# The 64x64 inverses of a gated DeltaNet block: lower quarter from 32x32 blocks stacked four to a tile

## The chip, the cores and the metric

The kernel runs on one core of a Trainium2 chip. The core's engines work side by side and meet through semaphores: PE (TensorE, the matrix products), DVE (VectorE), ACT (ScalarE), POOL (GpSimd) and SP (SyncE, which here only issues DMAs; ACT issues some too). The metric is the device time of one launch in microseconds (us); lower is better. All times here come from the runs and from one profiled execution of the kernel before.

## The reference

One residual block over a sequence of 1024 tokens of width 1024, in float32. With a condition vector c that gives six rows of shifts, scales and gates (`mod = silu(c) @ w_ada + b_ada`):

```
h = rms_norm(x, norm1_w) * (1 + scale1) + shift1
x = x + gate1 * (concat[gated_delta_net(h @ W_in), short_conv(h @ W_in)] @ w_out)
h = rms_norm(x, norm2_w) * (1 + scale2) + shift2
x = x + gate2 * ((silu(h @ w_gate) * (h @ w_up)) @ w_down)
out = rms_norm(x, norm_f_w)
```

The part that the change touches lies in the gated DeltaNet: 4 heads of 128 channels, the sequence cut into 16 chunks of 64 tokens. For each head and chunk

```
lmat = where(strict, (k_beta @ k.T) * decay, 0)            # 64 x 64, strictly lower
tmat = triangular_solve(lmat, eye, lower, unit_diagonal)   # inverse of (1 + lmat)
u = tmat @ v_beta
w = tmat @ (k_beta * exp(g))
```

and then a scan over the chunks carries a 128x128 state per head. With 1 + lmat written in 32x32 blocks, A11 and A22 on the diagonal and A21 below, the inverse has inv(A11) and inv(A22) on its diagonal and -inv(A22) A21 inv(A11) below it. That last block is the lower quarter of the title.

## The kernel before, in words

**Work on PE.** Nearly all products are float32 products made from pieces: a matrix is split into a rounded high part and a remainder, and three products of 128x128 by 128x512 (high by high, high by low, low by high) add up in one PSUM bank. These are the `acc<-h,u` products: the in-projection h @ W_in, eight steps of 128 of the contraction, three products each, for a column block of 128 and a half of the tokens (512). After the DeltaNet come W_out and the SwiGLU, from line L91 and L92 on.

**Two halves.** The DeltaNet runs twice, `gdn(hf)` for hf = 0 and 1, each for 512 tokens: 4 heads, and per head 4 tiles t of 128 tokens, each of which holds two chunks of 64 (c = 0, 1) side by side as a block-diagonal 128x128 matrix. In turn:

- `stage_a` per head: products of k with k give L (128x4x128: rows, tile, columns) with the sign already turned, so L holds minus lmat on its lower part and the diagonal blocks. It writes the sixteen 32x32 diagonal blocks of the head to a DRAM buffer `dl` by four DMAs, and multiplies L by the mask `offm` (L1134; in the profile `L<-L,ct`), which leaves only the block -A21 of each chunk.
- When all four heads are there, all 64 blocks are loaded into one tile A (a block per partition), inverted by a loop on DVE (L1232 to L1240), and written to the DRAM buffer `dx`: 64 rows of 1024, row h * 16 + 4 r + t for the diagonal position r and the tile t.
- `merge` per head (L1174): four DMAs put the inverted blocks of the head on the diagonal of `xbd[h]` (`xbd<-dx`); DVE transposes every 32x32 block (`Tt<-xbd`); P = L^T Tt, four products of 128 columns; an evacuation into L (`L<-P`, ACT); Q = xbd^T P, four products; DVE adds Q to Tt (`Tt<-Tt,Q`). Tt is then the transpose of tmat. DVE writes k times its factor into L (`L<-kt,bk`); u = Tt^T u and w = L^T Tt follow with their evacuations (`u<-u`, and WQ).
- The chain: for each tile and chunk the products A, K and O with the states S, and DVE and ACT work between them. Its first product is `K<-A,kt`. After it come the outputs, which end in the products `y<-ident,u`.

**What sets the order.** Up to `sim.run()` the work is written as tasks (a loader and splitter of weights, `fill`, which issues the acc products, the DeltaNet's tasks, `ada`, which makes the rows of `mod`, the evacuations). While the kernel is built, a planner (`Sim`) estimates when each instruction can start and orders tasks by priority (`merge` has 1, `fill` 9: acc products fill what is left). So the order of each engine's instructions is fixed at build time and not at run time; an engine runs its list in turn, and an instruction that isn't ready holds up all behind it. All instructions ordered this way carry the line L440 in the profile. Where a copy may go to ACT or DVE (`ecopy`) or a DMA to SP's or ACT's queue (`dma2`), the planner picks one. From L91 and L92 on the order is written by hand.

**Queues.** DMAs are issued by SP and ACT and use eight semaphores, DMAHW0 to DMAHW7, in turn over both queues: a DMA waits until the DMA that had its semaphore last has landed, and the DMAs queued behind it on the same engine wait too. Loads of weights go through a ring of five 256 KB buffers `raw` on SP; among them are those of w_ada, which DVE adds up eight in a row into `aacc` (`aacc<-raw,c_act,aacc`), ACT casts (`raw<-aacc`) and PE reduces (`ada<-raw,ones`).

Of the kernel before, what the change touches and what calls it, by code (L numbers as in the profile page):

```python
# [13 lines left out]
ALU = mybir.AluOpType  # L14
# [3 lines left out]
P = 128  # L18
# [35 lines left out]
def kernel(  # L54
# [25 lines left out]
    class Ordered:  # L80
# [18 lines left out]
    PE, DVE, ACT, POOL, SP = (Ordered(n, e) for n, e in (  # L99
        ("pe", nc.tensor), ("dve", nc.vector), ("act", nc.scalar), ("pool", nc.gpsimd), ("sp", nc.sync)))  # L100
# [30 lines left out]
    def v3(ap, a):  # L131
        return ap.rearrange("p (a b) -> p a b", a=a)

    def flat(ap):
        return ap.rearrange("p a b -> p (a b)")

    def bc2(col, n):
        return col.unsqueeze(2).to_broadcast([col.shape[0], col.shape[1], n])

    def bc1(row, n):  # L140
        return row.unsqueeze(1).to_broadcast([row.shape[0], n, row.shape[1]])
# [53 lines left out]
    def dma2(out, in_):  # L195
        kw = dict(out=out, in_=in_)
        mover[0].either([("sp", "dma_start", nc.sync.dma_start, (), kw), ("act", "dma_start", nc.scalar.dma_start, (), kw)])
# [98 lines left out]
    class Sim:  # L296
# [18 lines left out]
        def free(self, t):  # L315
            res, i = self.owner.pop(t.tensor.name)
            res.slots.append((max([a[4] for a in self.acc.get(t.tensor.name, [])] + [0.0]), i))
            res.slots.sort()
# [205 lines left out]
    tri, blk, mL, mU, offm = (ct[:, i * P:(i + 1) * P] for i in range(5))  # L524
# [16 lines left out]
    sim = Sim(seq, dict(pe=T_START[0], dve=T_START[1], act=T_START[2], pool=T_START[3], sp=T_START[4]))  # L541
# [8 lines left out]
    dense, chb = sim.res("b", 3), sim.res("b", 5, (6, 7, 3, 4, 5))  # L550
# [6 lines left out]
    def bank(res, name):  # L557
        return res.tile(psp, [P, HT], F32, name)

    def gt(tag, shape=(P, 4, P), dtype=F32):  # L560
        return GP[tag].tile(gp, list(shape), dtype, tag)
# [4 lines left out]
    free = sim.free  # L566

    def ecopy(dst, src):
        sim.either([("act", "copy", nc.scalar.copy, (dst, src), {}), ("dve", "tensor_copy", nc.vector.tensor_copy, (dst, src), {})])
# [9 lines left out]
    def mm(out_, lhsT, rhs, start=True, stop=True):  # L579
        PE.matmul(out_, lhsT, rhs, start=start, stop=stop)  # L580
# [5 lines left out]
    done = set()  # L586
# [483 lines left out]
    xbd, S = [], {}  # L1070
    sw = lambda ap: ap.rearrange("p t (c n) -> p t c n", c=2)
    tsl = lambda t: slice(t * P, (t + 1) * P)
# [21 lines left out]
    def stage_a(hf, h, dl, T, dec):  # L1094
# [5 lines left out]
        at, L, WQ, egl = (dec[h][n] for n in ("at", "L", "WQ", "egl"))  # L1100
# [30 lines left out]
        DVE.tensor_tensor(bv, rk, hcol("beta"), ALU.mult)  # L1131
        for t in (nk, rk, av, nav):
            free(t)
        DVE.tensor_tensor(L, L, bc1(offm, 4), ALU.mult)  # L1134
        DVE.tensor_tensor(qd, v3(qv, 4), qd, ALU.mult)
        pqk = bank(chb, "qk")
        for t in range(4):
# [36 lines left out]
    def merge(hf, h, T, dx):  # L1174
        st, t_ = sc_[hf], T[h]
        u = us[hf]
        for r in range(4):
            dma2(xbd[h][32 * r:32 * r + 32, :, 32 * r:32 * r + 32],
                dx[h * 16 + r * 4:h * 16 + r * 4 + 4, :].rearrange("t (a b) -> a t b", a=32))
        Tt = gt("Tt")  # L1180
        sim.wait(lambda: ("a", hf, h) in done)
        DVE.transpose(flat(Tt), flat(xbd[h]))
        pP = bank(chb, "P")
        for t in range(4):
            mm(pP[:, tsl(t)], t_["L"][:, t, :], Tt[:, t, :])
        ecopy(flat(t_["L"]), pP)
        free(pP)
        pQ = bank(chb, "Q")
        for t in range(4):
            mm(pQ[:, tsl(t)], xbd[h][:, t, :], t_["L"][:, t, :])  # L1190
        DVE.tensor_tensor(flat(Tt), flat(Tt), pQ, ALU.add)
        free(pQ)
        DVE.tensor_tensor(t_["L"], t_["kt"], bc2(t_["bk"], P), ALU.mult)
        free(t_["bk"])
        sim.wait(lambda: ("vt", hf, h) in done)
        pu = bank(chb, "u")
        for t in range(4):
            mm(pu[:, tsl(t)], Tt[:, t, :], u[:, h, t, :])
        ecopy(flat(u[:, h]), pu)
        free(pu)  # L1200
        pw = bank(chb, "w")
        for t in range(4):
            mm(pw[:, tsl(t)], t_["L"][:, t, :], Tt[:, t, :])
        free(t_["L"])
        free(Tt)
        ecopy(t_["WQ"].rearrange("p t (c n) -> p t c n", c=4)[:, :, 0:4:3, :],
                 pw.rearrange("p (t c n) -> p t c n", t=4, c=2))
        free(pw)
        DVE.tensor_tensor(t_["kt"], t_["kt"], bc2(st["kd"][:, :, h], P), ALU.mult)
        done.add(("uw", hf, h))  # L1210

    def gdn(hf):
# [10 lines left out]
        for h in heads:  # L1223
            sim.spawn(decays, PR["a"], hf, h, rows, dec)
            sim.spawn(stage_a, PR["a"], hf, h, dl, T, dec)
            sim.spawn(stage_v, PR["v"], hf, h, T)
# [17 lines left out]
        for h in heads:  # L1244
            sim.spawn(merge, PR["m"], hf, h, T, dx)
# [467 lines left out]
    c = {p: {} for p in range(NP)}  # L1713
# [435 lines left out]
```

## Time and profile before

| what | value |
|---|---|
| median of 3 runs (lowest to highest) | 1187.25 us (1186.67 to 1187.44) |
| the profiled execution's own time | 1186.41 us |
| its span in the trace | 1184.6 us |
| mean granted TensorE clock | 0.998 |
| PE busy | 1171.7 us (99%) |
| DVE, ACT, POOL busy | 928.4, 528.4, 55.6 us |
| merges of the first half, the second half | from about 196 us, from about 377 us |
| static order (L91, L92) begins | 490 us |

The median stands 0.84 us above the profiled execution, and 1.8 us of that execution's time lie outside its span.

How to read the lines below. A group of instructions reads: line, engine, operation, out<-in by the program's names (for a product 128*128 is the size of the stationary operand), partitions x elements and type, x count | busy us, mean ns of one | idle time of the engine just before them, and what ended most of it. A timeline row has the start, the time to the end of the last of its instructions, the engine and what ran. A product leaves one record for each pass, and a product in plain float32 has two passes. Records of PE overlap in its pipe, so the mean of one is more than the distance between two starts. A row by stretches gives for each engine busy time and instructions in that stretch, then the granted clock (PEclk), the DMA share and GB/s. A DMA row gives the queue, the number, KB each and the median us from issue to landing. A row of waits of PE reads: who waits <- for whom: us in total, times, the longest.

### The profile page before, as it was taken

What the parts mean: (1) busy time and instruction counts of PE and PEld (TensorE: products, weight loads), DVE (VectorE), ACT (ScalarE), POOL (GpSimd) and SP (SyncE); (2) the same over time, 40 slices, a digit from 0 to 9 for tenths busy, and PEclk for the clock granted to TensorE, in tenths of its full rate; (3) what the DMA queues carried; (4) which work ended last, traced back from release to release, by engine and by line L of the source; (5) the groups of instructions that cost most, each with busy time, mean ns of one, the idle gap of its engine ahead of it and who ended that gap; (6) DMA issues with size and microseconds to landing.
All of it is one profiled execution on the core that took longest, in us unless ns stands there. A gap on an engine that the chain in (4) does not pass through costs nothing.

```text
span 1184.6 us, 16797 instructions
## 1 busy us (share of the span) xinstructions
PE 1171.7 (99%) x5723; PEld 984.3 (83%) x5723; DVE 928.4 (78%) x1739; ACT 528.4 (45%) x1117; POOL 55.6 (5%) x95
## 2 busy tenths in 40 slices
PE   8999999999999999999999999999999999999997
PEld 7888888988888988888888888888888888888886
DVE  6998989799978789658787677767767697688676
ACT  3498732359642545125443333333333355433343
POOL 1010000001000001100000000000000000000003
PEclk9999999999999999999999999999999999999999
DMA  9934465544424546632354655455644679869413
GB/s 290 301 77 120 125 179 160 160 116 137 112 47 114 154 121 206 260 98 81 133 168 142 222 188 179 153 175 187 224 155 133 222 280 395 306 203 343 146 37 142
DMA packets 175775, 207.08 MB, mean 175 GB/s; under 512 B 21829, under 2 KB 107978, under 8 KB 175690
## 3 DMA queue, kind: packets, MB, share of 16 engines
q1 hardware_dynamic: 170312, 202.85, 53.7%
q10 hardware_dynamic: 5378, 3.16, 0.9%
q8 instruction: 45, 0.74, 0.3%
q14 instruction: 40, 0.33, 0.1%
HBM read 150.91 MB, written 55.05 MB: 174 GB/s over the span
## 4 chain that ended last, share of the span: by engine, by line
PE 95%; DVE 2%; DMA 1%; ACT 1%; issue 0%; SPq 0%; DVEq 0%; ACTq 0%
PE acc L91 34%; PE acc L440 26%; PE dn L91 17%; PE o L91 4%; PE o L440 4%; PE A L440 1%; PE K L440 1%; PE ab L440 1%; PE Q L440 1%; PE u L440 1%; PE w L440 1%; PE P L440 1%; PE kk L440 1%; PE qk L440 1%; DMA wr<-in_w_in_dram 1%; PE O L440 1%
## 5 line engine op out<-in xcount | busy, mean ns | idle before, releaser
L440 PE MATMUL acc<-h,u 128*128 128x512 f32 x1200 | 302.6, 398 | 0.0
L440 PEld LDWEIGHTS acc<-h,u 128*128 128x128 f32 x1200 | 219.0, 188 | 41.2
L91 PE MATMUL acc<-h,hl 128*128 128x512 f32 x600 | 140.1, 390 | 0.0
L91 PEld LDWEIGHTS acc<-h,hl 128*128 128x128 f32 x600 | 112.4, 188 | 23.2
L91 PE MATMUL acc<-h,u 128*128 128x512 f32 x456 | 106.1, 389 | 0.0
L91 PE MATMUL acc<-T,hl 128*128 128x512 f32 x432 | 101.3, 390 | 0.2 <-ACT cc L92 0.2
L91 PEld LDWEIGHTS acc<-h,u 128*128 128x128 f32 x456 | 85.6, 188 | 17.7
L91 PEld LDWEIGHTS acc<-T,hl 128*128 128x128 f32 x432 | 80.9, 188 | 17.2 <-ACT cc L92 0.6
L92 DVE TENSOR_TENSOR xo<-xo,dn 128x512 f32<-128x512 f32 x84 | 57.1, 684 | 44.1 <-PE dn L91 36.2
L91 PE MATMUL dn<-h,h 128*128 128x512 f32 x396 | 90.7, 389 | 0.0
L91 PEld LDWEIGHTS dn<-h,h 128*128 128x128 f32 x396 | 74.3, 188 | 15.4
L92 ACT COPY cc<-acc 128x512 f32<-128x512 f32 x66 | 38.4, 590 | 108.4 <-PE acc L91 108.4
L91 PE MATMUL acc<-T,u 128*128 128x512 f32 x360 | 84.0, 389 | 0.0
L91 PEld LDWEIGHTS acc<-T,u 128*128 128x128 f32 x360 | 67.6, 188 | 14.0
L440 ACT CAST u<-raw 128x512 fp32r<-128x512 f32 x64 | 39.8, 622 | 70.9 <-PE acc L440 61.1
L92 DVE TENSOR_TENSOR cc<-cc,acc 128x512 f32<-128x512 f32 x66 | 43.8, 683 | 29.8 <-PE acc L91 29.8
L440 DVE TENSOR_TENSOR u<-raw,u 128x512 fp32r<-128x512 f32 x82 | 56.1, 684 | 12.6 <-ACT u L440 11.8
L92 DVE TENSOR_TENSOR hl<-R,hl 128x512 fp32r<-128x512 f32 x60 | 39.4, 688 | 33.4 <-ACT hl L92 33.4
L440 DVE SCALAR_TENSOR_TENSOR cv<-pr,cols_b,cv 128x512 f32<-128x512 f32 x72 | 53.1, 746 | 1.3 <-ACT cv L440 0.9
L92 ACT CAST h<-rw 128x512 fp32r<-128x512 f32 x57 | 32.7, 617 | 41.0 <-PE dn L91 34.6
L92 ACT CAST hl<-R 128x512 fp32r<-128x512 f32 x60 | 35.7, 620 | 24.7 <-DVE R L92 10.7
L92 DVE TENSOR_TENSOR u<-R,u 128x512 fp32r<-128x512 f32 x46 | 30.1, 687 | 20.5 <-ACT u L92 20.5
(336 smaller groups left out, 2026.2 us busy)
## 6 DMA issues: line engine op xcount, KB each, us to landing
raw<-in_w_in_dram SPq DMA_DIRECT2D x82, 256.0 KB, 3.4
am_scr<-cc SPq DMA_DIRECT2D x77, 256.0 KB, 4.5
raw<-in_w_ada_dram SPq DMA_DIRECT2D x56, 256.0 KB, 3.3
rw<-am_scr SPq DMA_DIRECT2D x55, 256.0 KB, 5.1
rw<-bm_scr SPq DMA_DIRECT2D x53, 256.0 KB, 5.3
bm_scr<-raw SPq DMA_DIRECT2D x51, 256.0 KB, 5.5
R<-in_w_gate_dram SPq DMA_DIRECT2D x22, 512.0 KB, 4.3
R<-in_w_up_dram SPq DMA_DIRECT2D x22, 512.0 KB, 5.4
```

The costliest lines, as they stand in the source:

```text
L91: return call(*a, **k)
L92: ins = call(*a, **k)
L440: ins = call(*a, **k)
```

## The change

The mask of L in `stage_a` is gone: only the blocks -A21 are read from L now. A `merge` works with 32x32 blocks instead of block-diagonal 128x128 tiles:

- CB holds the blocks -A21, four on the diagonal of a 128x128 tile: chunks c = 0, 1 of the two tiles t = p + 2g, p = 0, 1. Two such tiles (g = 0, 1) make a head, written by four copies of 32x2x32 from L.
- Two DMAs bring the inverted A22 blocks into the columns 32 to 63 of L's first two tiles, stacked in the same way in the partition direction, and two DVE transposes of 128x32 turn them.
- Four DMAs bring the inverted A11 blocks on the diagonal of XA, as CB is; four DMAs fill X as `xbd[h]` was filled before.
- P is two products of 32 columns (CB stationary, the transposed A22 blocks moving); one copy of 128x64 brings it into L; Q is two products of 32 columns (XA stationary); four copies of 32x2x32 put Q's blocks into the upper right quarter of each chunk of Tt. Tt is DVE's transpose of X, and nothing is added to it.

A step and head thus has two products of 32 columns where it had four of 128, and ten DMAs where it had four. Heads h and h + 2 share the tiles `xbd[h % 2]` (X) and `xbd[2 + h % 2]` (XA and CB), so the merge of head h + 2 begins only after the products Q of head h are issued. In all, the built program has 5268 products instead of 5300, and 80 DMAs from dx instead of 32.

```diff
@@ -1131,7 +1131,6 @@
         DVE.tensor_tensor(bv, rk, hcol("beta"), ALU.mult)
         for t in (nk, rk, av, nav):
             free(t)
-        DVE.tensor_tensor(L, L, bc1(offm, 4), ALU.mult)
         DVE.tensor_tensor(qd, v3(qv, 4), qd, ALU.mult)
         pqk = bank(chb, "qk")
         for t in range(4):
@@ -1174,22 +1173,38 @@
     def merge(hf, h, T, dx):
         st, t_ = sc_[hf], T[h]
         u = us[hf]
+        X, L = xbd[h % 2], t_["L"]
+        XA, CB = xbd[2 + h % 2][:, 0:2, :], xbd[2 + h % 2][:, 2:4, :]
+        sim.wait(lambda: h < 2 or ("xb", hf, h - 2) in done)
+        slots_ = [(c, p, slice(32 * (2 * c + p), 32 * (2 * c + p) + 32)) for c in range(2) for p in range(2)]
+        for c, p, sl in slots_:
+            ecopy(CB[sl, :, sl], L[64 * c + 32:64 * c + 64, p:4:2, 64 * c:64 * c + 32])
+        for c in range(2):
+            dma2(L[64 * c:64 * c + 64, 0:2, 32:64],
+                 dx[h * 16 + 8 * c + 4:h * 16 + 8 * c + 8, :].rearrange("(g p) (a b) -> (p a) g b", p=2, a=32))
+        for c, p, sl in slots_:
+            r0 = h * 16 + 8 * c + p
+            dma2(XA[sl, :, sl], dx[r0:r0 + 3:2, :].rearrange("g (a b) -> a g b", a=32))
         for r in range(4):
-            dma2(xbd[h][32 * r:32 * r + 32, :, 32 * r:32 * r + 32],
+            dma2(X[32 * r:32 * r + 32, :, 32 * r:32 * r + 32],
                 dx[h * 16 + r * 4:h * 16 + r * 4 + 4, :].rearrange("t (a b) -> a t b", a=32))
+        for g in range(2):
+            DVE.transpose(L[:, 2 + g, 32:64], L[:, g, 32:64])
+        pP = bank(chb, "P")
+        for g in range(2):
+            mm(pP[:, 32 * g:32 * g + 32], CB[:, g, :], L[:, 2 + g, 32:64])
+        ecopy(L[:, 0:2, 96:128], v3(pP[:, 0:64], 2))
+        free(pP)
         Tt = gt("Tt")
+        DVE.transpose(flat(Tt), flat(X))
+        pQ = bank(chb, "Q")
+        for g in range(2):
+            mm(pQ[:, 32 * g:32 * g + 32], XA[:, g, :], L[:, g, 96:128])
+        done.add(("xb", hf, h))
+        for c, p, sl in slots_:
+            ecopy(Tt[64 * c:64 * c + 32, p:4:2, 64 * c + 32:64 * c + 64], v3(pQ[sl, 0:64], 2))
+        free(pQ)
         sim.wait(lambda: ("a", hf, h) in done)
-        DVE.transpose(flat(Tt), flat(xbd[h]))
-        pP = bank(chb, "P")
-        for t in range(4):
-            mm(pP[:, tsl(t)], t_["L"][:, t, :], Tt[:, t, :])
-        ecopy(flat(t_["L"]), pP)
-        free(pP)
-        pQ = bank(chb, "Q")
-        for t in range(4):
-            mm(pQ[:, tsl(t)], xbd[h][:, t, :], t_["L"][:, t, :])
-        DVE.tensor_tensor(flat(Tt), flat(Tt), pQ, ALU.add)
-        free(pQ)
         DVE.tensor_tensor(t_["L"], t_["kt"], bc2(t_["bk"], P), ALU.mult)
         free(t_["bk"])
         sim.wait(lambda: ("vt", hf, h) in done)
```

The orders below name each tile with its number. In the first half P_423 and so on are results of P, L_221 to L_224 the L tiles of heads 0 to 3, xbd2 and xbd3 hold XA and CB, and raw_N are weight loads. First PE, from where P of head 0 stands, before:

```order
L440 MATMUL acc_415_2237<-h7_1_181_1000,u_392_2083 128x512 x3
L440 MATMUL acc_426_2296<-h0_0_45_272,u_404_2160 128x512 x3
L440 MATMUL acc_426_2296<-h1_0_53_333,u_404_2160 128x512 x3
L440 MATMUL P_427_2300<-Tt_420_2264,L_221_1185 128x128 x4
L440 MATMUL acc_426_2296<-h2_0_60_377,u_404_2160 128x512 x2
L440 MATMUL P_430_2315<-Tt_423_2281,L_222_1186 128x128 x4
```

and after:

```order
L440 MATMUL acc_419_2251<-h7_1_181_1000,u_395_2090 128x512 x3
L440 MATMUL P_423_2299<-L_221_1185,xbd2_1049 128x32 x2
L440 MATMUL acc_426_2310<-h0_0_45_272,u_407_2164 128x512 x3
L440 MATMUL acc_426_2310<-h1_0_53_333,u_407_2164 128x512 x3
L440 MATMUL Q_429_2327<-L_221_1185,xbd2_1049 128x32 x2
L440 MATMUL acc_426_2310<-h2_0_60_377,u_407_2164 128x512 x2
L440 MATMUL P_430_2335<-L_222_1186,xbd3_1050 128x32 x2
```

P of head 0 moved ahead of six acc products; the merges of the four heads that stood close together now stretch over 29 acc products, up to the product w of head 2, whose place is:

```order
L440 MATMUL acc_446_2461<-h0_1_138_793,u_407_2164 128x512
L440 MATMUL u_448_2470<-u_297_1522,Tt_439_2421 128x128 x3
L440 MATMUL acc_446_2461<-h0_1_138_793,u_407_2164 128x512
L440 MATMUL acc_446_2461<-h1_1_143_808,u_407_2164 128x512 x2
L440 MATMUL w_450_2489<-Tt_439_2421,L_223_1187 128x128 x4
```

This w reads L_223 (head 2), and u_448 reads Tt_439, head 2's Tt.

SP's queue at the same place, before, with what each DMA waits for in brackets (the engines' names stand for their semaphores):

```order
L440 DMA xbd2_1049<-dx_213_1169 32x4x32 [waits DMAHW4_49]
L440 DMA xbd3_1050<-dx_213_1169 32x4x32 [waits DMAHW6_49,Pool_49]
L440 DMA xbd3_1050<-dx_213_1169 32x4x32 [waits DMAHW0_49]
L440 DMA raw_422_2278<-in_w_in_dram 128x4x128 [waits DMAHW1_49,PE_49,Activation_49]
L440 DMA raw_421_2272<-in_w_ada_dram 128x512 [waits DMAHW2_49,Activation_49]
```

and after, from the last DMA of SP's first wave (heads 0 and 1) into the second wave (heads 2 and 3):

```order
L440 DMA xbd1_1048<-dx_213_1169 32x4x32 [waits DMAHW5_49]
L440 DMA raw_424_2302<-in_w_in_dram 128x4x128 [waits DMAHW7_49,DMAHW0_49,DVE_49]
L440 DMA raw_422_2277<-in_w_ada_dram 128x512 [waits DMAHW0_49]
L440 DMA raw_431_2337<-in_w_in_dram 128x4x128 [waits DMAHW2_49,DMAHW1_49,DVE_49]
L440 DMA L_223_1187<-dx_213_1169 64x2x32 [waits DMAHW3_49]
L440 DMA L_223_1187<-dx_213_1169 64x2x32 [waits DMAHW5_49]
L440 DMA xbd2_1049<-dx_213_1169 32x2x32 [waits DMAHW7_49,DMAHW6_49,PE_49]
L440 DMA xbd2_1049<-dx_213_1169 32x2x32 [waits DMAHW1_49]
L440 DMA xbd0_1047<-dx_213_1169 32x4x32 [waits DMAHW2_49,DVE_49]
L440 DMA xbd0_1047<-dx_213_1169 32x4x32 [waits DMAHW3_49]
L440 DMA raw_435_2381<-in_w_ada_dram 128x512 [waits DMAHW5_49]
L440 DMA L_224_1188<-dx_213_1169 64x2x32 [waits DMAHW6_49]
```

Three rows further, SP's queue after the change ends the second wave and goes on with weight loads:

```order
L440 DMA xbd3_1050<-dx_213_1169 32x2x32 [waits DMAHW4_49]
L440 DMA xbd1_1048<-dx_213_1169 32x4x32 [waits DMAHW5_49,DVE_49]
L440 DMA xbd1_1048<-dx_213_1169 32x4x32 [waits DMAHW6_49]
L440 DMA raw_441_2429<-in_w_ada_dram 128x512 [waits DMAHW7_49]
L440 DMA raw_447_2463<-in_w_ada_dram 128x512 [waits DMAHW0_49,DVE_49]
L440 DMA raw_449_2482<-in_w_ada_dram 128x512 [waits DMAHW1_49,DVE_49]
```

The small DMAs that followed one another before now have weight loads between them and take turns with them on the eight semaphores: xbd2's first waits for raw_424 on DMAHW7, its second for raw_431 on DMAHW1, xbd1's first for raw_435 on DMAHW5.

DVE at the place where head 2's L is filled, before:

```order
L440 TENSOR_TENSOR kt_274_1387<-kt_274_1387,kd_203_1118 128x512
L440 TENSOR_TENSOR Tt_424_2289<-Tt_424_2289,Q_438_2362 128x512
L440 TENSOR_TENSOR L_223_1187<-kt_290_1469,bk_320_1626 128x512
L440 TENSOR_TENSOR Tt_428_2303<-Tt_428_2303,Q_442_2381 128x512
L440 TENSOR_TENSOR L_224_1188<-kt_336_1731,bk_354_1800 128x512
L440 SCALAR_TENSOR_TENSOR aacc_416_2245<-raw_444_2394,c_act_112,aacc_416_2245 128x512
```

and after:

```order
L440 STREAM_TRANSPOSE Tt_444_2453<-xbd1_1048 128x512
L440 SCALAR_TENSOR_TENSOR aacc_415_2217<-raw_441_2429,c_act_112,aacc_415_2217 128x512
L440 TENSOR_TENSOR L_223_1187<-kt_284_1460,bk_316_1605 128x512
L440 TENSOR_TENSOR cv_420_2259<-acc_426_2310,cv_420_2259 128x512
L440 SCALAR_TENSOR_TENSOR aacc_415_2217<-raw_447_2463,c_act_112,aacc_415_2217 128x512
L440 TENSOR_TENSOR L_224_1188<-kt_332_1701,bk_349_1768 128x512
```

Steps of aacc, which read weight loads, moved ahead of the filling of L for heads 2 and 3.

In the second half ACT's order after the change has, near the merge of heads 2 and 3:

```order
L440 COPY L_557_2963<-P_777_4309 128x2x32
L440 CAST h5_0_774_4275<-raw_762_4216 128x512
L440 COPY u_654_3440<-u_779_4327 128x512
L440 COPY Tt_781_4334<-Q_782_4336 32x2x32 x2
L440 COPY WQ_564_2970<-w_786_4353 128x4x2x64
```

The cast of raw_762, a load of y from scratch memory on SP, stands between an evacuation of P and the copies of u and Q.

## The prediction

> **What bounds the kernel now.** I read four views in this order: the page's busy times, busy time by stretch of the span, the waits of PE, then PE's groups and timeline in the stretch that the change touches.
>
> ```profile
> PE 1171.7 (99%) x5723; PEld 984.3 (83%) x5723; DVE 928.4 (78%) x1739; ACT 528.4 (45%) x1117; POOL 55.6 (5%) x95
> 60.00:480.00 420.00, 420.00 (x2281) 359.68 (x2280) 369.56 (x853) 230.48 (x578) 29.04 (x33) 1.00 0.47 134
> PE acc L91 <- ACT cc L92: 0.2, 1, 0.2
> ```
>
> PE is busy for 99% of the span, and from 60 to 480 us, where both halves' merges lie, for all 420 us at a granted clock of 1.00. Its waits from 60 to 600 us are one of 0.2 us. So PE's instruction stream is the time: what the change takes from PE counts fully, and what it adds on DVE (370 of those 420 us busy), ACT (230) or the DMA queues counts only where PE comes to wait. The sum therefore has two kinds of term: PE time saved, and new PE waits.
>
> **PE time saved.** The two products of a merge, and the nearest rows to a narrow product:
>
> ```profile
> L440 PE MATMUL P<-Tt,L 128*128 128x128 f32 x64 | 8.8, 275 | 0.0
> L440 PE MATMUL Q<-L,xbd 128*128 128x128 f32 x64 | 8.4, 275 | 0.0
> 341.10 41.55 PE L440 MATMUL acc<-h,u 128*128 128x512 f32 x182
> 382.49 2.84 PE L440 MATMUL P<-Tt,L 128*128 128x128 f32 x24
> 385.16 1.95 PE L440 MATMUL Q<-L,xbd 128*128 128x128 f32 x16
> 96.05 0.52 PE L440 MATMUL G<-g,ct 128*128 128x16 f32 x4
> 96.41 0.31 PE L440 MATMUL abt<-ident,raw 128*128 128x128 f32 x1
> 11.12 1.02 PE L440 MATMUL ada<-c_act,wa 128*128 128x1 f32 x8 [0.36 <-DMA wa<-in_w_ada_dram]
> 12.01 0.91 PE L440 MATMUL tr<-ident,x 128*128 128x128 f32 x4
> ```
>
> Records overlap in the pipe, so I price them by the distance between starts. Each fp32 product of 128 columns leaves two records. 24 records of P take 385.16 - 382.49 = 2.67 us, 0.111 each, so the 128 records removed are worth 14.2 us. The 64 new ones (two products, two passes, two steps, eight merges) have 32 moving columns but still 128 stationary ones. The rows on both sides of 32 columns are G with 16 (four records in 0.36 us, 0.09 each) and, as the upper end, P itself with 128 (0.111); ada with one column pays that too (eight in 0.89). So 5.8 to 7.1 us stay, and 7.1 to 8.4 are saved. I take 7.1: one column costs as much as 128 in two of these three rows, and the narrow products stand scattered between acc products.
>
> The Trainium skill ("TensorE: Matmul & The Clock Gate", "Back-to-back issue gap") gives products of 1 to 64 columns a gap of about 25 ns, and its section "LDWEIGHTS (loading the stationary operand)" about 107 ns for any load of 128 stationary columns. The rows above agree with the second. By the first, the 64 records would be an estimated 1.6 us and the saving 12.6.
>
> **Work off PE.** DVE loses eight masks and eight additions and gains 16 transposes of 128x32; ACT's eight evacuations of P shrink, and some 65 copies of 32x2x32 and 48 small DMAs are added.
>
> ```profile
> L440 DVE TENSOR_TENSOR L<-L,ct 128x512 f32<-128x512 f32 x8 | 5.5, 686 | 1.0 <-DMA dl<-L 0.9
> L440 DVE TENSOR_TENSOR Tt<-Tt,Q 128x512 f32<-128x512 f32 x8 | 5.5, 682 | 1.7 <-PE Q L440 1.7
> L440 DVE COPY ablo<-abt 128x32 f32<-128x32 f32 x2 | 0.4, 182 | 0.0
> L440 ACT COPY L<-P 128x512 f32<-128x512 f32 x8 | 4.7, 588 | 10.3 <-PE P L440 10.3
> L440 ACT COPY S<-K 128x128 f32<-128x128 f32 x4 | 0.8, 280 | 1.7 <-PE K L440 1.7
> ```
>
> DVE: 16 x 0.68 = 11 us less; 16 transposes and some ten copies at about 0.18 (ablo, 32 columns) are 4.7 more. ACT: 55 copies between 0.18 and 0.28 (S) are 10 to 15 us more, 8 x about 0.3 less for the smaller L<-P, and 24 issues at 0.46 (SP's rate, below) are 11 more. DVE's slack of 50 us and ACT's of 190 from 60 to 480 hide this as work. Its cost, if any, is lateness inside a merge.
>
> **New waits, first half.** Here the DMAs decide. T0 is the landing of dx.
>
> ```profile
> 193.03 0.46 SPq L440 DMA_DIRECT2D dx<-A  x1
> 196.06 4.14 SPq L440 DMA_DIRECT2D xbd<-dx  x9
> dx<-A SPq DMA_DIRECT2D x1, 256.0 KB, 2.9
> xbd<-dx SPq DMA_DIRECT2D x9, 16.0 KB, 1.9
> raw<-in_w_in_dram SPq DMA_DIRECT2D x82, 256.0 KB, 3.4
> raw<-in_w_ada_dram SPq DMA_DIRECT2D x56, 256.0 KB, 3.3
> 200.93 1.05 PE L440 MATMUL P<-Tt,L 128*128 128x128 f32 x8
> 201.73 0.71 PE L440 MATMUL acc<-h,u 128*128 128x512 f32 x2
> L440 DVE SCALAR_TENSOR_TENSOR aacc<-raw,c_act,aacc 128x512 f32<-128x512 f32 x49 | 36.5, 744 | 3.2 <-DMA raw<-in_w_ada_dram 3.0
> L440 DVE TENSOR_TENSOR L<-kt,bk 128x512 f32<-128x512 f32 x8 | 5.5, 683 | 0.0
> 218.93 1.05 PE L440 MATMUL K<-A,kt 128*128 128x128 f32 x8
> ```
>
> T0 = 193.03 + 2.9 = 195.9. Before, all 16 small DMAs go out at once (nine on SP at 4.14 / 9 = 0.46 each), and P of head 0 starts at T0 + 5.0. In the new order six acc products fewer stand ahead of it; one costs 41.39 / 182 = 0.227, so PE reaches it at T0 + 3.6, when the A22 blocks, in the first DMAs after dx, have had 1.9 us to land and been transposed.
>
> Now the DMAs come in two waves, since heads 2 and 3 reuse the tiles of heads 0 and 1, and the rows of SP in the part on the change show what lies between: 256 KB weight loads. A DMA waits for the landing of the one eight before it. SP's first wave (ten at 0.46) ends at T0 + 4.6. Then raw_424, raw_422 and raw_431 go out at 4.7, 5.2 and 5.7 and two blocks of L_223 by 7.0. The first xbd2 row waits for raw_424 (4.7 + 3.4 = 8.1), the next for raw_431 (9.1). xbd0 twice to 10.8, raw_435 at 10.9, L_224 and xbd3 to 13.3; xbd1 waits for raw_435 (10.9 + 3.3 = 14.2), and raw_441 goes out behind it at 15.1 and lands at 18.4. DVE's order has aacc<-raw_441 (0.74) ahead of L_223<-kt,bk (0.68), which w of head 2 reads: ready at 19.8. From P(0) to that w PE has 29 acc products (6.6 us), 20 products u and w of 128 columns (40 x 0.111 = 4.4) and 16 narrow ones (3.0): due at 3.6 + 14.0 = 17.6. **PE waits about 2.3 us there**, for a weight load that has nothing to do with the merge. Behind it the same chain runs once more (raw_449, aacc, a cast to raw, copies of u, A), and I allow 0.7 for it:
>
> ```profile
> L440 ACT CAST raw<-aacc 128x512 fp32r<-128x512 f32 x6 | 3.7, 618 | 4.5 <-DVE aacc L440 2.4 <-issue 1.8 <-DVE pr L440 0.4
> L440 ACT COPY u<-u 128x512 f32<-128x512 f32 x8 | 4.7, 587 | 5.1 <-PE u L440 5.0
> ```
>
> First half: 3.0 us, between 0 (loads a little quicker, or fillers that reach) and 7.2 (the last rival).
>
> **Second half.** Here the merge meets loads of y from scratch memory. The nearest load from scratch memory is:
>
> ```profile
> Tt<-z_scr SPq DMA_DIRECT2D x3, 256.0 KB, 4.7
> ```
>
> T0' is the second dx's landing. On SP raw_762 stands behind the first wave and waits of the same kind and goes out by my count at T0' + 10.5; it lands 4.7 later, at 15.2. ACT's order has its cast (0.62) ahead of a copy of u (0.59) and of copies of Q into Tt (two of about 0.2), so the last is done at 16.8, and u of head 2 needs it at 15.7 to 16.4. I take 0.5, between 0 (a load at 3.3) and 3.3 (below).
>
> The Trainium skill (the same page, "Part 1: The HAM clock gate") says that PE falls to half clock after an idle window of about 3.4 us. The stretch above has 1.00 with no such idle, so no run here shows it; a wait of 3.0 us would be near that bound, and one beyond it would cost an estimated 2 to 4 us more at half speed.
>
> Last, the end of this part: the chain's last O, the last y and the first product of the static order.
>
> ```profile
> 445.49 1.05 PE L440 MATMUL O<-A,at 128*128 128x128 f32 x8
> 462.18 0.60 PE L440 MATMUL y<-ident,u 128*128 128x128 f32 x4
> 490.41 0.40 PE L91 MATMUL o<-L,WQ 128*128 128x512 f32 x1
> ```
>
> 28 us lie between y and the static order, full of products that don't need the chain, so a chain that is some us late is not waited for there.
>
> **Sum.** -7.1 + 3.0 + 0.5 = -3.6 us. Against the profiled execution's own 1186.41 us that is 1182.8; the median of the runs is 0.84 above that execution, so **1183.6 us** against 1187.25.
>
> **Rivals.**
> - *The waits are covered.* For it: before, PE waited 0.0 at P and Q although the loads share the queues. Then 1187.25 - 7.1 = 1180.2, or 1178.9 with G's price. Against: raw_441 didn't stand in a merge before.
> - *The waits eat the saving*: 4 to 7 us of them, 1184.9 to 1188.
> - *Loads in series are slow; slower than before.* Place: the weight loads that the second wave waits for. The loads of z_scr in that very stretch took 4.7 us. At 4.7 instead of 3.3 each of the three in series in the first half adds 1.4, 3.0 + 4.2 = 7.2 us; two in the second half make 0.5 + 2.8 = 3.3. Together 10.5, 1187.25 - 7.1 + 10.5 = 1190.6. It decides from a mean wait of 3.55 us per half (no gain), and is visibly slower from 4.75. Against: 138 of these loads took 3.3 to 3.4 as the median.
> - *Narrow products cost almost nothing.* Against it stand the rows of ada and G, which pay 0.09 to 0.11 for one and 16 columns. If a record took a quarter of G's 0.09, 64 would be 1.4, the saving 12.8, and with the waits 1187.25 - 12.8 + 3.5 = 1177.9. The first rule of the Trainium skill named above would make it so.
>
> **How the numbers follow.** 0.2% of this kernel, 2.4 us, is about what a measurement can tell from no change: faster is below 1184.9, slower above 1189.6. Chances: the forecast (waits of 1 to 5 us in all, 1181 to 1185.2) 0.45; covered (about 1180) 0.24; eaten (1185 to 1189) 0.13; slower 0.15; narrow products nearly free 0.03. Faster holds 0.03, 0.24 and a part of the forecast's 0.45, some 0.37: 0.64. Slower is the fourth, 0.15; the rest, 0.21, lies between. The range 1179 to 1188.5 leaves out the fast end of two cases (0.05) and the slower one (0.15).
>
> **What the profile after would show.** P and Q with 64 records, the distance between starts of adjacent ones 0.09 to 0.111. PE waits between 190 and 222 us, the longest at w or u of heads 2 and 3, released by DVE's L<-kt,bk or ACT's u copy, whose own wait is for raw<-in_w_ada_dram. Elsewhere no new waits. Wrong would I be if xbd DMAs land far later than 1.9 us, if PE waits at P or Q of heads 0 and 1, if the granted clock falls below 1.00 in that stretch, or if the difference lies after 490 us.

## The result, and the profile after

The changed kernel takes 1187.82 us in the median of 13 runs (1186.21 to 1188.93), the kernel before 1187.75 us in runs beside it. The ratio is 1.0001 with a 95% interval of 0.9994 to 1.0008, so by the interval the change moves the time by something between -0.7 and +0.9 us. The forecast was 1183.6, faster by 3.6 us. The products did get cheaper by about what was reckoned; all of it was given back.

First the changed kernel's page and its busy time by stretches:

```profile
PE 1170.2 (99%) x5659; PEld 978.0 (83%) x5659; DVE 928.2 (78%) x1763; ACT 527.0 (44%) x1157; POOL 56.2 (5%) x95
```

```profile
60.00:480.00 420.00, 417.30 (x2220) 352.61 (x2219) 367.56 (x877) 229.99 (x619) 31.00 (x32) 1.00 0.47 134
```

PE's waits from 60 to 600 us, where there was one of 0.2 us before:

```profile
PE P L440 <- DVE L L440: 1.5, 3, 0.9
PE Q L440 <- ACT L L440: 0.7, 2, 0.4
PE y L440 <- DVE u L440: 0.2, 1, 0.2
PE w L440 <- DVE L L440: 0.2, 1, 0.2
PE acc L91 <- ACT cc L92: 0.2, 1, 0.2
```

PE has 64 records fewer and stands idle for 2.7 us of a stretch in which it had never been idle. The groups of the two products, after (before, they are in the prediction):

```profile
L440 PE MATMUL Q<-L,xbd 128*128 128x32 f32 x32 | 4.6, 262 | 0.7 <-ACT L L440 0.7
L440 PE MATMUL P<-L,xbd 128*128 128x32 f32 x32 | 4.5, 264 | 1.6 <-DVE L L440 1.5
```

P and Q fell from 17.2 us busy to 9.1. Busy time counts tails that overlap in the pipe, so I also added up, over the trace from the first acc product to the static order, the distance from each record of PE to the next start. P and Q have 13.9 us before and 6.8 after, 7.1 less. The records that are the same in both kernels have 6.3 more: acc 3.0, w 1.2, o 0.9, the others 1.3 together. PE's waits stand in these distances (one at P lies in the distance of the acc product ahead of it).

Most of the 6.3 us is lateness, and it is more than the rows of waits show. From 60 to 484 us PE stops eleven times, where before it never did. Set against the median distance of records with the same neighbours, the distances that hold a stop are 4.6 us longer: 2.7 that the profile counts as idle and 1.9 more, some 0.17 at each stop. Distances without an idle time are another 1.8 us longer than before, and the profile names no wait for those. The switches between plain float32 and acc products, which cut up the merges now (before, their products stood in rows of 8 to 24 records), are not what costs: there are 202 of them before and 208 after in that stretch. By the medians the record ahead of a plain float32 product takes 0.233 us for 0.227 and the first plain one behind it 0.108 for 0.111; on the way back the last plain one takes 0.031 for 0.112 and the first acc product behind it 0.315 for 0.227. Together that is 0.01 us.

Where the time stands in each kernel can be read from three points: the two writes of dx on SP, which end the two solves, and PE's first product of the static order. Before, then after:

```profile
193.03 0.46 SPq L440 DMA_DIRECT2D dx<-A  x1
373.80 0.47 SPq L440 DMA_DIRECT2D dx<-A  x1
490.41 0.40 PE L91 MATMUL o<-L,WQ 128*128 128x512 f32 x1
```

```profile
193.47 0.47 SPq L440 DMA_DIRECT2D dx<-A  x1
373.17 0.48 SPq L440 DMA_DIRECT2D dx<-A  x1
490.26 0.40 PE L91 MATMUL o<-L,WQ 128*128 128x512 f32 x1
```

| stretch | before, us | after, us | difference |
|---|---|---|---|
| start to the first dx | 193.03 | 193.47 | +0.44 |
| first dx to second dx (first merges) | 180.77 | 179.70 | -1.07 |
| second dx to the static order (second merges) | 116.61 | 117.09 | +0.48 |
| static order to the end of the span | 694.19 | 694.44 | +0.25 |

The three points cut PE's list a little differently in the two kernels: after the change three acc products more and one of ada fewer start between the two writes, and one acc product fewer behind the second. With 0.24 us for each, the same products gained 1.5 us in the first half and lost 0.7 in the second, where each half was to save half of 7.1. So 2.0 us of that were given back in the first half and 4.3 in the second. In the second half PE's longest waits in the merges are, in the timeline of the changed kernel:

```profile
383.53 0.63 PE L440 MATMUL Q<-L,xbd 128*128 128x32 f32 x4 [0.41 <-ACT L L440]
390.75 0.60 PE L440 MATMUL P<-L,xbd 128*128 128x32 f32 x4 [0.85 <-DVE L L440]
395.23 0.60 PE L440 MATMUL P<-L,xbd 128*128 128x32 f32 x4 [0.39 <-DVE L L440]
```

DVE at that time:

```profile
389.84 0.43 DVE L440 CAST h<-raw 128x512 fp32r<-128x512 f32 x1
390.39 0.30 DVE L440 STREAM_TRANSPOSE L<-L 128x32 f32<-128x32 f32 x2
...
394.87 0.30 DVE L440 STREAM_TRANSPOSE L<-L 128x32 f32<-128x32 f32 x2 [1.77 <-DMA L<-dx]
```

And the queues of ACT (the first row) and SP:

```profile
383.38 0.61 ACTq L440 DMA_DIRECT2D L<-dx  x1
383.49 1.01 SPq L440 DMA_DIRECT2D raw<-in_w_in_dram  x2
385.32 0.59 SPq L440 DMA_DIRECT2D L<-dx  x1
388.43 1.85 SPq L440 DMA_DIRECT2D xbd<-dx  x4
391.28 1.24 SPq L440 DMA_DIRECT2D L<-dx  x2
```

P of head 2 (390.75) and P of head 3 (395.23) wait for the transposes of their A22 blocks, and both times the transposes start 0.02 us after the later of the two DMAs that bring the blocks has landed. By the marks of the DMAs' semaphores in the trace, SP's DMA of 385.32 landed at 390.37, and the second of the two of 391.28 at 394.85. DVE had been free for 0.1 us when the first of these landed, so it isn't its casts that PE waited for. What was late is the small DMAs themselves: all DMAs issued from 383.4 to 385.4 us, three loads of 256 KB and five small ones of the second wave, took 4.6 to 5.2 us to land. SP stood from 385.9 to 388.4 because its next DMA waited for the semaphore of one of these small ones (ACT's of 383.38, landed at 388.36), and so the blocks of head 3 left SP only at 391.28. The DMAs from issue to landing in the stretch 373 to 400, in medians:

```profile
raw<-in_w_in_dram SPq DMA_DIRECT2D x5, 256.0 KB, 5.0
L<-dx SPq DMA_DIRECT2D x5, 16.0 KB, 2.8
L<-dx ACTq DMA_DIRECT2D x3, 16.0 KB, 5.0
```

In the first half, the place that the prediction had worked out is there too: w of head 2 at 216.58, with T0 = 196.4 (the start of the first DMA from dx) at T0 + 20.2 where 19.8 was forecast, released by DVE's L, which follows the step of aacc that waited for a load (PE, then DVE):

```profile
216.58 1.16 PE L440 MATMUL w<-Tt,L 128*128 128x128 f32 x8 [0.17 <-DVE L L440]
```

```profile
215.17 0.75 DVE L440 SCALAR_TENSOR_TENSOR aacc<-raw,c_act,aacc 128x512 f32<-128x512 f32 x1 [0.84 <-DMA raw<-in_w_ada_dram]
215.84 0.68 DVE L440 TENSOR_TENSOR L<-kt,bk 128x512 f32<-128x512 f32 x1
```

PE's wait there is 0.17 us and not 2.3, because PE itself was late: from P of head 0 to its arrival at this w it took 16.2 us (200.20 to 216.41) where 14.0 were reckoned. Of the 2.2 us more, 0.56 are its waits at Q of head 0 and P of head 3; the rest are longer distances between records.

### The profile page after: what moved, and what is told of

It reads as the page before. It is cut to its first block, busy times and chain, and to the rows that moved or that the text cites. A ratio compares the mean times of both kernels' runs of the same rounds, so it can differ in the third digit from the quotient of the medians.

```text
span 1184.7 us, 16801 instructions
## 1 busy us (share of the span) xinstructions
PE 1170.2 (99%) x5659; PEld 978.0 (83%) x5659; DVE 928.2 (78%) x1763; ACT 527.0 (44%) x1157; POOL 56.2 (5%) x95
## 4 chain that ended last, share of the span: by engine, by line
PE 86%; DVE 5%; DMA 4%; ACT 1%; issue 1%; ACTq 1%; SPq 0%; POOL 0%; DVEq 0%; POOLq 0%
PE acc L91 34%; PE acc L440 21%; PE dn L91 17%; PE o L91 4%; PE o L440 3%; DMA raw<-in_w_out_dram 1%; DMA raw<-in_w_in_dram 1%; DVE raw L440 1%; DMA xbd<-dx 1%; PE ada L440 1%; PE ab L440 1%; PE K L440 1%; PE qk L440 1%; PE kk L440 1%; DMA raw<-in_w_ada_dram 1%
## 5 line engine op out<-in xcount | busy, mean ns | idle before, releaser
L91 PEld LDWEIGHTS acc<-T,hl 128*128 128x128 f32 x432 | 80.9, 188 | 17.2 <-ACT cc L92 0.6
L440 ACT CAST u<-raw 128x512 fp32r<-128x512 f32 x60 | 37.2, 623 | 57.3 <-PE acc L440 50.3
```

The source lines that it names most:

```text
L91: return call(*a, **k)
L440: ins = call(*a, **k)
```

## The experiments

All were timed against the kernel before on the same chip (5 to 12 runs of each); the microseconds are the ratio's distance from 1 times 1187. Waits are those of one profiled execution, which can lie up to 2.2 us from the median of its kernel (1184.26 against 1182.07 in the first run below). The 4.4 us of waits in the changed kernel's merges that some expectations name come near to the 4.6 by distances above; by the rows of waits, as given below, they are 2.4. Theory W: the narrow products save what was reckoned, and what the new transfers and copies make late in the merges gives it back. Rivals: N, narrow products save little; A, ACT's queue is to blame; S, what counts is the order that the planner builds, and switching between kinds of products.

**The narrow products alone.** The kernel before, with

```diff
-        for t in range(4):
-            mm(pP[:, tsl(t)], t_["L"][:, t, :], Tt[:, t, :])
-        ecopy(flat(t_["L"]), pP)
+        for g in range(2):
+            mm(pP[:, 32 * g:32 * g + 32], t_["L"][:, g, :], Tt[:, g, 32:64])
+        ecopy(flat(t_["L"]).rearrange("p (a b) -> p a b", b=64), bc1(pP[:, 0:64], 8))
```

and the like for Q and the addition.

> The kernel before with P and Q cut to two products of 32 columns each and nothing else changed: masks, DMAs, copies and additions keep their sizes (they read the 64 columns eight times over), so the kernel leaves three quarters of both products out. Theory W (the narrow products save PE 6 to 7.4 us, and the waits that the new transfers and copies bring into the merges, 4.4 us in the changed kernel's trace, and some smaller ones give it back): 6 to 7 us faster than before, 1181 to 1182, and PE waits in the merges under 1 us. Rival N (the narrow products save little, since each still loads 128 stationary columns and stands alone among acc products): no more than 2 us faster, and the changed kernel's waits are beside the point.

Ratio 0.9959 (0.9947 to 0.9971): 4.9 us faster, 3.4 to 6.3. P and Q cost as in the changed kernel, with no wait before them:

```profile
L440 PE MATMUL Q<-L,xbd 128*128 128x32 f32 x32 | 4.6, 261 | 0.0
L440 PE MATMUL P<-Tt,L 128*128 128x32 f32 x32 | 4.5, 262 | 0.0
```

N falls. The gain is below the 6 to 7 expected: the profiled execution has about 1.5 us of new waits elsewhere (two for the states' S at A, one each at K, ada and w).

**Everything but the narrowness.** The changed kernel with four products of 128 columns:

```diff
-            mm(pP[:, 32 * g:32 * g + 32], CB[:, g, :], L[:, 2 + g, 32:64])
+            for r in range(2):
+                mm(pP[:, tsl(2 * r + g)], CB[:, g, :], L[:, 2 + g, :])
```

> The changed kernel with four products of 128 columns again for P and for Q, of the same stacked operands, of which the same blocks as before are used; its DMAs, copies and transposes are untouched. 64 more records at 0.111 and 64 dearer by 0.005 are 7.4 us more work on PE. Theory W: the waits end when data arrive, so part of the added work fills them: 3 to 6 us slower than the changed kernel, 1191 to 1194, with waits in the merges of 1 to 3 us. Rival N: within 2 us of the changed kernel.

Ratio 1.0045 (1.0033 to 1.0057): 5.3 us slower than before, 3.9 to 6.8. Its waits:

```profile
PE P L440 <- DVE L L440: 1.4, 2, 1.1
PE u L440 <- DVE Tt L440: 0.5, 1, 0.5
PE ada L440 <- ACT raw L440: 0.4, 1, 0.4
```

With the run before it this splits the change, the planner's order of each included: the narrow products bring 4.9 us, the stacking (48 more DMAs, two waves, some 65 copies, 16 transposes) costs 5.3, and both together were measured as 0.1 slower.

**The mask alone.** The kernel before without `DVE.tensor_tensor(L, L, bc1(offm, 4), ALU.mult)`.

> The kernel before without the mask of L and with nothing else of the change, so that the products P read unmasked blocks of L. Theory W: DVE isn't the bound, eight instructions of 0.69 us less on it are worth nothing by themselves; the planner builds a somewhat other order, which may move the time by up to 1.5 us either way: 1185.5 to 1188.5. Rival S (what the changed kernel loses comes from the order that the planner builds whenever costs change a little): this one moves by 2 us or more as well.

Ratio 0.9996 (0.9988 to 1.0005), PE never idle in the merges. DVE's saved work is worth nothing, as priced; a small change of the order did no harm here.

**All small DMAs on SP.** In `merge`, `dma2(` became `dma(` throughout.

> The changed kernel with all ten DMAs of a merge on SP's queue, none on ACT's. Rival A (the waits come from ACT: its evacuations of P and Q stand behind the ten DMA issues in its own queue, 0.39 and 0.53 us at Q of head 0): those two waits vanish and the time falls by 1 to 2.5 us to 1185.5 to 1187. Theory W (it is the landing of the second wave of small DMAs, late because they take turns with weight loads): SP has twice the issues, 0.46 to 0.6 us each, the second wave lands later still, and the time stays or rises by up to 3 us, 1187.5 to 1191.

Ratio 1.0069 (1.0055 to 1.0083), 8.2 us slower. The wait at Q went, and eight others came:

```profile
PE A L440 <- DVE S L440: 1.7, 3, 0.9
PE K L440 <- DVE A L440: 1.4, 2, 0.9
PE P L440 <- DVE L L440: 1.1, 2, 0.6
PE O L440 <- ACT A L440: 1.1, 1, 1.1
PE acc L440 <- ACT u L440: 0.9, 1, 0.9
```

So A was right about the wait and wrong about the time: with 17 or 18 more issues on SP in each half, PE waits in the chain (A, K, O) and once at an acc product for its weights. Part of the 8.2 us is the clock. Behind the waits in the chain the granted clock (the number ahead of the DMA share) was at half for 6.8 us:

```profile
445.30:448.70 3.40, 1.57 (x11) 1.14 (x10) 3.40 (x8) 2.24 (x4) 0.00 (x0) 1.00 0.99 269
448.70:452.20 3.50, 2.44 (x10) 1.93 (x11) 3.42 (x7) 1.06 (x3) 0.00 (x0) 0.51 1.04 414
452.20:455.60 3.40, 3.40 (x13) 3.01 (x13) 3.17 (x6) 2.99 (x14) 0.00 (x0) 0.50 0.98 372
```

PE was busy for 2.44 + 3.40 us there; at full clock that work would have taken about half, so the estimate is up to 2.9 us in this execution.

**Later landings in the plan.** The planner's rule for a DMA of a merge:

```diff
                     end = rd = self.pipe + DMA_T[1]
+                    if task["name"] == "merge":
+                        end = rd = end + 1.5
```

> The changed kernel, built with the planner told that every DMA of a merge lands 1.5 us later than it reckoned, so that it puts more acc products ahead of P and Q; no instruction is added or removed. Theory W: the waits in the merges fall from 4.4 us to 1 or 2, and the time to 1184 to 1186. Rival S (the saving is lost to switching between fp32 products and acc products, and to the order elsewhere, not to waits in the merges): unchanged, 1187 to 1189.

Ratio 0.9985 (0.9977 to 0.9994), 1.8 us faster than before. The sign is W's, but not the reason given: the profiled execution has 4.3 us of waits in the merges, more than the 2.4 of the changed kernel, at Q, w and u instead of P (at 1186.68 it stands 1.2 us above the median of its runs):

```profile
PE Q L440 <- ACT L L440: 1.7, 1, 1.7
PE w L440 <- DVE L L440: 1.6, 1, 1.6
PE u L440 <- DVE Tt L440: 1.0, 1, 1.0
```

The control with 0.5 in place of 1.5:

> A control: the changed kernel, built with the planner told that the DMAs of a merge land 0.5 us later than it reckoned (1.5 in the earlier run). The order of the merges and of what lies between them changes, the work does not. If the orders of the runs with later landings gained because they wait for real landings: between the changed kernel and the run with 1.5, 1185.5 to 1187.5. If any new order moves the time by chance (as the run with P's evacuation on DVE suggests, 3 to 4 us above the one that it was made from): anything from 1183 to 1190, with waits in other places than those of the changed kernel.

Ratio 0.9988 (0.9979 to 0.9997), 1.4 us faster, between the two as the first branch has it; its interval overlaps that of 1.5, so the two can't be told apart. Its waits (P 1.5, u 1.9, y 0.4, Q 0.3) stand in part at other places than the changed kernel's, as the second branch has it. So a gain by chance of the order isn't ruled out.

**One wave.** Each head has its own XA and CB, X's blocks land in Tt:

```diff
-        X, L = xbd[h % 2], t_["L"]
-        XA, CB = xbd[2 + h % 2][:, 0:2, :], xbd[2 + h % 2][:, 2:4, :]
-        sim.wait(lambda: h < 2 or ("xb", hf, h - 2) in done)
+        L = t_["L"]
+        XA, CB = xbd[h][:, 0:2, :], xbd[h][:, 2:4, :]
+        Tt = gt("Tt")
+        POOL.memset(Tt, 0.0)
...
-            dma2(X[32 * r:32 * r + 32, :, 32 * r:32 * r + 32],
+            dma2(Tt[32 * r:32 * r + 32, :, 32 * r:32 * r + 32],
...
-        DVE.transpose(flat(Tt), flat(X))
+        DVE.transpose(flat(Tt), flat(Tt))
```

> The changed kernel without the sharing of tiles between heads h and h + 2: each head has its own tile for XA and CB, and the blocks of X land in Tt itself (set to zero by POOL before), which DVE transposes in place. All 40 small DMAs of a half go out at once, ahead of the weight loads. If the waits come from the second wave of DMAs taking turns with loads: those at P of heads 2 and 3 go, PE waits 1 to 2 us in all in the merges, and the time is 1183 to 1185.5. If they come from the small DMAs as such (20 issues of 0.5 to 0.6 us on each queue, ahead of loads and copies): no faster than the changed kernel, 1186.5 to 1190.

Ratio 0.9982 (0.9973 to 0.999), 2.1 us faster. The A22 blocks land earlier, in the same stretch from 373 to 400 us:

```profile
L<-dx SPq DMA_DIRECT2D x4, 16.0 KB, 2.2
L<-dx ACTq DMA_DIRECT2D x4, 16.0 KB, 2.1
```

And the waits at P are gone:

```profile
PE ada L440 <- ACT raw L440: 1.3, 1, 1.3
PE y L440 <- DVE so L440: 1.0, 1, 1.0
PE Q L440 <- ACT L L440: 0.5, 2, 0.3
```

Those at ada and y, 2.3 us, lie outside the merges; the changed kernel had 0.2 at y.

**One wave and later landings** (both edits).

> One wave as above, and the planner told that the DMAs of a merge land 1.5 us later than it reckoned. If the rest of the waits is the planner's too early landing: 1 to 2 us below the run with one wave, 1181.5 to 1184. If not: the same within 1 us, as the later order of the changed kernel gained only 1 to 2 us.

Ratio 0.9971 (0.996 to 0.9981), 3.4 us faster, median 1183.99: the best of all runs with the whole computation, and better than both kernels. Waits at Q 1.2 and u 0.3.

**Transposed blocks from DRAM.** One wave, with

```diff
+        for k, b_ in enumerate((tmp, gt("Tt", (64, 512)))):
+            DVE.tensor_copy(b_.rearrange("p (a b) -> p a b", a=16), A[:, :, 16 * k:16 * k + 16].rearrange("p a b -> p b a"))
+            dma(dt_[:, 512 * k:512 * k + 512], b_)
```

and the merges' transposes taken out.

> One wave as in the run with own tiles, and DVE's transposes gone too: after the solve DVE writes the transposed blocks once (two copies of 64x512) to a second DRAM buffer, from which A22 and Tt's blocks are read already transposed. If DVE's place in the chain from landing to P and u (transposes behind casts of late loads) makes waits of its own, they vanish: 1181.5 to 1184, below the run with one wave by 1 to 2 us. If the landing alone decides, the two copies and one more DMA of 2.9 us put everything later by about 2 us while acc products fill the time: equal to the run with one wave within 1 us.

Ratio 1.001 (1.0001 to 1.0019), 1.2 us slower than before and 3.3 slower than one wave: the later landing is not covered; PE waits 2.4 us at u and 1.7 at Q. Neither branch had it that bad. Taking the transposes off DVE gained nothing here, which fits the trace above, where they started as soon as the blocks had landed.

**Copies in place of six DMAs.** One wave, with A22 and A11 copied from X by `ecopy`; then the same with later landings.

> The run with one wave, but six of a merge's ten DMAs replaced by copies inside SBUF: only X's four blocks are read from DRAM (16 small DMAs in a half, as in the kernel before), and A22 and A11 are copied from them by eight copies of 32x2x32 on ACT or DVE. If the number of small DMAs is what costs (issue time on ACT ahead of its evacuations, weight loads pushed back by 20 issues on SP): 1 to 3 us below the run with one wave, 1181.5 to 1183.5. If the copies, 0.2 us each and in the chain from landing to P, cost as much as they save: 1184 to 1187, with the waits now at P for ACT's or DVE's copies.

> The same with copies, and the planner told that the DMAs of a merge land 1.5 us later than it reckoned. If the planner's estimate of landings still makes PE wait: 0.5 to 1.5 us below the run with copies alone. If not: the same within 1 us.

Ratios 0.9998 (0.9989 to 1.0008) and 0.9999 (0.9991 to 1.0008). As many small DMAs as the kernel before had, and no gain: PE's waits in the merges are 0.4 and 0.2 us, but others stand at ada, A, K and y (1.5 and 2.7 us), and the first has a stretch at half clock (last section); the granted clock of its runs is lower as a whole (table below). So these two settle neither whether the number of DMAs costs by itself nor whether the copies cost as much as they save.

**P's evacuation on DVE.** In the run with one wave and later landings, `ecopy` of P became `DVE.tensor_copy`.

> One wave with the later landings, and the evacuation of P always on DVE. If PE's wait at Q (1.2 us in that run's trace) comes from ACT's queue, where the evacuation stands behind DMA issues: it goes, and the time is 0.5 to 1.5 us below the run with one wave and later landings (1183.99), 1182.5 to 1183.5. If the wait comes from P itself, or DVE is as late: the same within 0.5 us.

Ratio 1.0005 (0.9997 to 1.0014), 4 us slower than the run it was made from by the two ratios, which are of two chips. Neither branch had that time. The wait at Q did go; in its place stand two of 1.2 us at u, for which the profile names nothing that PE waited for, and 2.8 us at A, ada and o. So that wait did come from ACT's queue, and removing it gained nothing that these runs show.

**The clock in all of them.** Each run has its mean granted clock, and it is not the same for all variants. If PE is busy all the time, a mean lower by 0.001 is an estimated 1.2 us of a span of 1185. The means over the runs that differ by 0.0007 and more from those of the kernel before beside them:

| run | its clock | the kernel before | worth by estimate, us | whole difference measured, us |
|---|---|---|---|---|
| all small DMAs on SP | 0.9957 | 0.9971 | +1.7 | +8.2 |
| later landings | 0.9978 | 0.9971 | -0.8 | -1.8 |
| one wave | 0.9977 | 0.9970 | -0.9 | -2.1 |
| one wave, later landings | 0.9980 | 0.9970 | -1.2 | -3.4 |
| copies | 0.9959 | 0.9977 | +2.1 | -0.2 |
| P's evacuation on DVE | 0.9967 | 0.9977 | +1.1 | +0.6 |

So up to 2.4 of the 4 us between the runs with and without P's evacuation on DVE can be the clock, and the copies alone may have saved some 2 us that the clock took back. The first two experiments, which split the change, differ from the kernel before by no more than 0.0003 in clock.

## Why the prediction was right or wrong

The measured time lies in the stated range, on the rival "the waits eat the saving" (0.13) and not on the forecast (0.45): the forecast gain of 3.6 us did not come, and it is the width of the range, not the sum, that holds the measured time. Step by step:

- *PE is the bound, and its idle time is the price.* Right: DVE's saved work moved nothing (the run without the mask; ACT's work was not varied alone), and idle time of PE appeared.
- *PE time saved, 7.1.* Right in size. The distances added up above went from 13.9 to 6.8 us. The lower price of 0.09 from G was a misreading: its four records stand 0.03, 0.11, 0.11 and 0.11 us apart, so products of 16 columns pay what those of 128 do, as ada's single column did.
- *Where PE would wait.* Wrong. Forecast were u or w of heads 2 and 3, the longest wait in the first half. PE waited at Q of head 0 in both halves (0.27 and 0.41 us), which the prediction itself named as a sign of being wrong, and longest at P of head 2 in the second half (0.85). The other sign came too: small DMAs that land far later than the 1.9 us reckoned with.
- *P of head 0 at T0 + 3.6.* Measured 200.20 - 196.4 = 3.8.
- *First half, 3.0 of waits.* The loss was 2.0 us, 0.7 of it in the rows of waits. The ready time of w of head 2 was worked out as T0 + 19.8 and its start measured as T0 + 20.2, so the chain of loads was followed rightly. But PE came there at T0 + 20.0 and not at 17.6, after waits of 0.27 to 0.29 at Q and P that the walk hadn't found; the loss lay spread before the place. That the sum came out near is in part luck.
- *Second half, 0.5 of waits (0 to 3.3).* This is the term that failed: 4.3 us were lost, beyond its upper bound. I followed one load to the copies of u and Q, and let the small DMAs land as fast as in the profile before (1.9 us). Among the loads that the second wave takes turns with they took 4.6 to 5.2, and the A22 blocks, DVE's transposes and P waited for that. The loads of w_in took 5.0 us there, beyond the 4.7 of the slower rival's condition; in the first half, where the same rival put 7.2, they took 3.1.
- *Narrow products nearly free, loads slow in both halves.* Neither came.
- *Handover to the static order.* Right: it starts 0.15 us earlier and isn't waited for.

That the narrowness is worth about 5 us and that the stacking costs as much is shown by the first two runs. That the sharing of tiles, through the late second wave, is a part of that cost is shown by the trace (landings of 5 us, then the waits at P) and borne out by one wave, in which both are gone; how many of its 2.1 us are due to it is not shown, since a changed plan alone gave 1.4 to 1.8 us and the clock may account for 0.9. Not settled either: how much of what is left in each variant is due to its own dependencies, and how much to the order that the planner happened to build. The runs with P's evacuation on DVE and with copies had waits in the merges removed, and showed others at other places.

## What to carry to other kernels

Where one engine is busy all the time, price a change by two sums: what its stream gets shorter by, and what new lateness stops it; the second can be as large while PE has less work and the other engines hardly more. Small transfers that go out among large loads can land as late as the loads do (5 us here in place of 2): issue them in one wave ahead, price their landing among the loads and not alone, and follow every block to its first reader, not only the slowest-looking one. Where differences are of a few us, compare the granted clock of the runs before explaining them. Where a planner sets the order, the untouched neighbours change too, so compare them before and after.

## What the runs showed of the hardware

The clock went to half with PE hardly idle. In the run with copies, the stretches around a dense row of narrow products (the numbers ahead of the DMA share are the granted clock):

```profile
383.40:386.90 3.50, 3.26 (x26) 3.09 (x26) 3.29 (x12) 3.26 (x16) 0.00 (x0) 1.00 0.81 265
386.90:390.30 3.40, 3.40 (x17) 3.30 (x16) 3.34 (x7) 2.65 (x9) 0.00 (x0) 0.50 0.25 80
```

PE's longest wait there, and the products at half clock:

```profile
385.15 0.60 PE L440 MATMUL P<-L,xbd 128*128 128x32 f32 x4 [0.24 <-DVE L L440]
387.17 2.34 PE L440 MATMUL u<-u,Tt 128*128 128x128 f32 x10
```

PE was busy for 3.26 of the 3.50 us before the drop, its longest wait there was 0.24 us, and most of its records were of 32 columns. Then ten records of u took 2.12 us (387.17 to the next start at 389.29), 0.21 each, where they take 0.11. This differs from the rule of the Trainium skill ("TensorE: Matmul & The Clock Gate", "Part 1: The HAM clock gate") of at least one idle window of about 3.4 us, as the prediction used it: here a window without such an idle was enough, and the measurement decides. In the run with all small DMAs on SP, too, the drop followed a window with 1.57 of 3.40 us busy in which no single wait was longer than 1.1 us. The length of the stretch, 3.4 us, agrees with that section of the Trainium skill. That the narrow products are the reason is argued, not shown; no run varied them alone at that place.

The changed kernel's profile has such a stretch at its start, where the profiled execution before had none (first before, then after):

```profile
16.90:20.30 3.40, 2.93 (x14) 2.27 (x15) 3.19 (x7) 0.73 (x2) 0.00 (x0) 1.00 1.17 304
```

```profile
16.90:20.30 3.40, 3.27 (x9) 2.48 (x10) 3.23 (x7) 0.14 (x2) 0.00 (x0) 0.50 1.15 301
```

It lies ahead of all that the change touches. At 17.0 us PE was 0.04 us earlier after the change than before, and at 27 us 0.61 later (the same row of 14 acc products starts at 26.94 and at 27.55), so the 0.44 us of the first stretch in the table above come from there.
